# A hybrid attention and mLSTM layer on one core: the second branch gate as one group of seven half-size products

## The chip, the cores and the metric

One core of one Trainium2 chip runs the whole kernel in one launch. The metric is the device time of one execution in microseconds (us), as the median of the runs. TensorE (PE) multiplies matrices; VectorE (DVE) and ScalarE (ACT) do the elementwise work and empty TensorE's accumulators in PSUM; GpSimd (POOL) and SyncE (SP) issue DMAs here.

## The reference

One layer of a decoder with two token mixers, sequence 512, model width 1024, fp32. Cut to what matters here:

```python
u  = rms_norm(h, norm_mix_g)
z  = u @ w_in                 # q,k,v | mLSTM q,k | v | output gate ob | i, f | ga | gb
ya = moba_attention(...)      # 8 heads x 64
hb = mlstm_chunkwise(...)     # 4 heads x 128
hb = hb * rsqrt(mean(hb*hb) + EPS)           # head norm
yb = sigmoid(ob) * hb * mlstm_norm_g
merged = sigmoid(ga) * (ya @ w_proj_a) + sigmoid(gb) * (yb @ w_proj_b)
h = h + merged @ w_out
h = h + swiglu(rms_norm(h, norm_ffn_g))
out = rms_norm(h, norm_final_g)
```

The branch gates `ga` and `gb` are each 512 tokens x 1024 features, a product of `u` with 1024 columns of `w_in`.

## The kernel before

Everything is held with features on the 128 partitions and the 512 tokens along the row. An fp32 product is made of three matmuls on numbers that are split into a high part (fp32r) and a low remainder: wh·h, wl·h, wh·l. For `u` the parts are the tiles `uh` and `ul`, eight of each; the row scale of the first norm, `rb`, is applied to the products afterwards.

**Units.** The weights of the projections come in units of 128x1024 (512 KB). For each unit SP loads `raw` (L195), ScalarE copies it to `wh` (L157) and VectorE subtracts to get `wl` (L170); `split_unit` runs two units ahead of the products (`LOOK`). `fill` takes the next unit and calls `run[kind]`. The kinds stand in a fixed order: q, k, va, ob, vb, qkb, ob, then eight units `ga`, eight `gb`, eight `p` (the two branch projections), eight `wo`. A unit of `ga`, `gb` or `wo` is 24 matmuls of 128x512 into one PSUM buffer (`mm3`, L210 to L212, eight feature tiles by three products).

**Buffers in PSUM.** `mmb` gives the projection's buffers (named mm), `sb` those named s, `accb` those named acc. The steps of attention and mLSTM (scores, masks, head norms) lie between the units; a scheduler sets each engine's order by priorities.

**The gates.** `run_g` empties a product: `ga` by a ScalarE copy, `gb` by a VectorE multiply with `rb` (L561). `run_p` makes the two projections of one block of 128 features in two PSUM buffers; VectorE multiplies each with its gate (L588, L589), adds them (L592), and the sum is split to `mgh` and `mgl`. `gate(m)` (L574 and the two sigmoids on ScalarE) prepares the gates of the block that follows. `run_wo` multiplies the merged blocks with `w_out`.

**The head norm of mLSTM.** `ml_d1` copies the numerator from PSUM to `nsb` on VectorE (L1673), and squares it on ScalarE; `ml_d2` sums the squares over the partitions by two matmuls into an s buffer, scales by 2^-39 on VectorE (L1684), takes exp(-0.5 ln) on ScalarE and one Newton step on VectorE (L336 to L338).

**Weight sums for the feed-forward part.** There, products are made in Winograd's form: a 2x2 block product by seven instead of eight block products, with sums of weight blocks. Some sums are made in DRAM, each by a copy (SP, L720) and an accumulating DMA (POOL, L722), in the order of `sum_steps`; `make_sums(n)` issues them up to a count that `fill` gives for each unit. While `st["hold"]` is true (attention steps 12 to 20) none are issued. POOL also loads the mLSTM rows `R` of each head (L1603), which are read by VectorE at L1615.

## Time and profile before

| | us |
|---|---|
| median of 3 runs (lowest, highest) | 715.43 (714.92, 715.52) |
| the profiled execution | 715.64 |
| its span, first to last instruction | 713.6 |
| PE busy | 703.6, x3272 |
| DVE busy | 600.0, x986 |
| ACT busy | 438.0, x746 |
| POOL busy | 69.8, x97 |
| mean granted clock of TensorE | 0.997 |

The span is what the instructions cover; 2.04 us of the profiled execution's own time lie around it. Matmuls are pipelined: a row of 128x512 shows 0.39 us, while the next one starts 0.23 us after it. So a busy PE in a slice says that matmuls followed one another, and the distance from start to start says how fast. The same holds, with smaller differences, for VectorE and ScalarE. In the timeline a bracket at a row's end gives the idle time of the engine before it and what ended it. The span from 254.42 us to 300.10 us is the stage of the second gate; the `p` units follow, and the `wo` units start at 343.62 us.

### The profile page before, as it was taken

The page shows a single profiled execution, that of the slowest core. Times are in us where ns is not written, and L with a number is a line of the kernel's source. Part 1 is how long each engine was busy: PE and PEld are TensorE (multiplying, and loading weights), DVE is VectorE, ACT ScalarE, POOL GpSimd, SP SyncE. Part 2 cuts the span into 40 slices and gives each one's busy share as a digit, 9 for nine tenths or more (in the row PEclk, how much of TensorE's full clock was granted, in tenths as well). Part 3 has the DMA queues.
Part 4 walks back from the last instruction along what each step waited for, and adds up shares of the span by engine and source line. Part 5 has one row for each costly group of instructions (what it writes and reads, how often), then busy time and mean ns, then how long its engine had stood idle before and what let it go on. Part 6 is the DMA issues. An engine that isn't in the chain of part 4 may idle for free.

```text
span 713.6 us, 9515 instructions
## 1 busy us (share of the span) xinstructions
PE 703.6 (99%) x3272; PEld 585.8 (82%) x3272; DVE 600.0 (84%) x986; ACT 438.0 (61%) x746; POOL 69.8 (10%) x97
## 2 busy tenths in 40 slices
PE   9999999999999999999999999999999999999995
PEld 6888888887888888888888888888888888888884
DVE  6788977888998578666699887898999799797996
ACT  6634888668784446723354756566675666575665
POOL 0013010000001000000020110011002004003000
PEclk9999999999999999999999999999999999999998
DMA  9759685623159997989988667669569649869703
GB/s 326 290 189 242 207 219 173 199 78 151 60 204 244 277 297 218 275 258 269 265 253 198 218 196 216 233 178 302 198 187 278 226 136 220 312 158 272 217 0 119
DMA packets 47009, 152.69 MB, mean 214 GB/s; under 512 B 5837, under 2 KB 6229, under 8 KB 42481
## 3 DMA queue, kind: packets, MB, share of 16 engines
q1 hardware_dynamic: 36880, 117.33, 47.7%
q0 software_dynamic: 9792, 34.21, 23.5%
q8 instruction: 26, 0.43, 0.2%
q10 hardware_dynamic: 288, 0.56, 0.2%
q14 instruction: 23, 0.18, 0.1%
HBM read 130.00 MB, written 53.52 MB: 257 GB/s over the span
## 4 chain that ended last, share of the span: by engine, by line
PE 82%; DVE 12%; ACT 3%; issue 2%; DVEq 0%; ACTq 0%
PE mm L212 10%; PE mm L210 10%; PE mm L211 10%; PE mm L855 5%; PE mm L856 5%; PE mm L854 5%; PE s L855 3%; PE s L856 3%; PE s L854 3%; PE mm L1104 2%; PE mm L1102 2%; PE mm L1101 2%; PE mm L315 2%; PE acc L315 2%; PE acc L856 1%
## 5 line engine op out<-in xcount | busy, mean ns | idle before, releaser
L157 ACT ACTIVATE w<-raw 128x1024 fp32r<-128x1024 f32 (+2 forms) x107 | 108.1, 1023 | 47.7 <-PE mm L855 20.0
L829 DVE TENSOR_TENSOR w<-raw,w 128x1024 fp32r<-128x1024 f32 x70 | 84.4, 1219 | 21.3 <-ACT w L157 21.0
L157 ACT ACTIVATE wh<-raw 128x1024 fp32r<-128x1024 f32 x56 | 59.0, 1054 | 61.4 <-PE mm L211 58.7
L170 DVE TENSOR_TENSOR wl<-raw,wh 128x1024 fp32r<-128x1024 f32 x56 | 68.2, 1218 | 10.2 <-ACT wh L157 10.0
L854 PE MATMUL mm<-w,bq 128*128 128x512 f32 x160 | 62.2, 389 | 0.0
L855 PE MATMUL mm<-w,bq 128*128 128x512 f32 x160 | 62.2, 389 | 0.0
L856 PE MATMUL mm<-w,bq 128*128 128x512 f32 x160 | 62.2, 389 | 0.0
L210 PE MATMUL mm<-u,wh 128*128 128x512 f32 x128 | 50.3, 393 | 0.0
L211 PE MATMUL mm<-u,wl 128*128 128x512 f32 x128 | 50.0, 391 | 0.0
L212 PE MATMUL mm<-u,wh 128*128 128x512 f32 x128 | 50.0, 390 | 0.0
L212 PE MATMUL mm<-ul,wh 128*128 128x512 f32 x128 | 49.8, 389 | 0.0
L211 PE MATMUL mm<-uh,wl 128*128 128x512 f32 x128 | 49.8, 389 | 0.0
L210 PE MATMUL mm<-uh,wh 128*128 128x512 f32 x128 | 49.8, 389 | 0.0
L854 PEld LDWEIGHTS mm<-w,bq 128*128 128x128 f32 x160 | 30.0, 188 | 6.3
L855 PEld LDWEIGHTS mm<-w,bq 128*128 128x128 f32 x160 | 30.0, 188 | 6.3
L856 PEld LDWEIGHTS mm<-w,bq 128*128 128x128 f32 x160 | 30.0, 188 | 6.2
L1010 DVE TENSOR_TENSOR w<-raw,w 128x1024 fp32r<-128x1024 f32 x25 | 30.2, 1216 | 1.4 <-ACT w L157 1.0
L1102 PE MATMUL mm<-w,ac 128*128 128x512 f32 x80 | 31.2, 389 | 0.0
L1101 PE MATMUL mm<-w,ac 128*128 128x512 f32 x80 | 31.1, 389 | 0.0
L854 PE MATMUL s<-w,bq 128*128 128x512 f32 x80 | 31.1, 389 | 0.0
L855 PE MATMUL s<-w,bq 128*128 128x512 f32 x80 | 31.1, 389 | 0.0
L856 PE MATMUL s<-w,bq 128*128 128x512 f32 x80 | 31.1, 389 | 0.0
(438 smaller groups left out, 1917.1 us busy)
## 6 DMA issues: line engine op xcount, KB each, us to landing
raw<-in_wall_dram SPq DMA_DIRECT2D x56, 512.0 KB, 5.6
raw<-in_wgc_dram SPq DMA_DIRECT2D x30, 512.0 KB, 5.1
raw<-ws SPq DMA_DIRECT2D x30, 512.0 KB, 5.8
ws<-in_wgc_dram SPq DMA_DIRECT2D x10, 1024.0 KB, 6.9
ws<-in_wgc_dram POOLq DMA_DIRECT2D x10, 1024.0 KB, 9.3
raw<-in_wds_dram SPq DMA_DIRECT2D x15, 512.0 KB, 6.6
ws<-in_wds_dram SPq DMA_DIRECT2D x10, 512.0 KB, 7.3
ws<-in_wds_dram POOLq DMA_DIRECT2D x10, 512.0 KB, 6.7
```

Source lines behind the costliest of these rows:

```text
L157: return A.activation(out_, in_, func, **kw)
L170: V.tensor_tensor(l, src, f(h), op=ALU.subtract)
L210: st["mm"] = T.matmul(ps, wh[:, c], rh[j], start=start and j == 0, stop=False)
L211: T.matmul(ps, wl[:, c], rh[j], start=False, stop=False)
L212: T.matmul(ps, wh[:, c], rl[j], start=False, stop=stop and j == n - 1)
L829: V.tensor_tensor(l, t, f(h), op=ALU.subtract)
L854: st["mm"] = T.matmul(ps[t], bh, wh[:, d], start=first and k == 0, stop=False, skip_group_check=not first)
L855: T.matmul(ps[t], bh, wl[:, d], start=False, stop=False, skip_group_check=not first)
L856: T.matmul(ps[t], bl, wh[:, d], start=False, stop=k == 3, skip_group_check=not first)
L1010: V.tensor_tensor(w[k][1], g[k], f(w[k][0]), op=ALU.subtract)
L1101: T.matmul(ps, bh, wh[:, d], start=first and k == 0, stop=False, skip_group_check=not first)
L1102: T.matmul(ps, bl, wh[:, d], start=False, stop=False, skip_group_check=not first)
```

## The change

**The second gate.** The eight units `gb` become fourteen units `gs`, two for each of the products W11, S1, S2, W12, S3, S4, W22 of one Winograd group on blocks of half size (512 features of `u` by 512 columns, 256 tokens). A unit is 12 matmuls of 128x512 (L633 to L635), where the two halves of the tokens are stationary and the weights move, so the gate comes out with tokens on the partitions. The sums S1 to S4 of the weights are made in DRAM from the new input `wgb`: four more copies on SP and four more accumulates on POOL, at the head of `sum_steps`. `hold` is gone, and the count given to `make_sums` is another function of the unit.

**The sums of `x`.** POOL loads `x` again (`load_x`, two DMAs of 1 MB, step 20), `combine` forms the sums of its blocks (step 25: for each of four pairs one ScalarE scaling and four VectorE steps of 128x256), and `recast` overwrites a half of `uh` and `ul` after the first unit of W11, S1, S2 and W12 (each four ScalarE and four VectorE steps of 128x256).

**Out of PSUM.** The products W11, S1 and S2 are copied to SBUF by ScalarE with their scale (`rt`, `nrt`), two copies each; W12, S3 and S4 are added to these by VectorE (L658, two each); W22 is copied by ScalarE. Each of the eight results is transposed in 32x32 blocks on VectorE (L659). After S4, and again after W22, POOL writes the four transposed row groups to DRAM (L663) and reads four blocks of `gb` back (L669), which puts the features on the partitions again.

**The p units** come in the order 4, 5, 6, 7, 0, 1, 2, 3 (`PORD`). The sums of the first three are copied from PSUM by ScalarE (two copies each), and their merging is done after the third.

**The head norm.** The copy to `nsb` moves to ScalarE, the scaling by 2^-39 goes into the scale of Ln and of the Newton step, and the last head's sum of squares lies in an mm buffer.

The diff, cut:

```diff
-    u += [("gb", m) for m in range(8)]
-    u += [("p", m) for m in range(8)]
+    u += [("gs", i) for i in range(2 * len(GW))]
+    u += [("p", m) for m in PORD]
...
-            while wstate["split"] <= min(u + LOOK, NGEN - 1):
+            kind, i = UNITS[u]
+            while wstate["split"] <= min(u + LOOK + (kind == "gs"), NGEN - 1):
                 split_unit()
             pos[0] += 1
-            make_sums(st["made"] if st["hold"] else min(st["made"] + 2, 6 * (u - 17) // 7))
+            v = u if u < G0 else max(u + G0, 2 * u - 2 * len(GW)) // 2
+            make_sums(5 * (min(v, G0 + 4) - 19 + max(v - G0 - 10, 0)) // 4)
...
+    def load_x():
+        for n, c in (("A", slice(0, 4)), ("B", slice(4, 8))):
+            gs[n] = slot4(name="c" + n)
+            nc.gpsimd.dma_start(gs[n], xT[c].rearrange("k p s -> p k s"))
...
+    def combine():
+        for k in range(4):
+            x, v = gs["A"][:, k], gs["B"][:, k]
+            ng = ng1[:, k : k + 1]
+            with tc.issue_after(raw_ins(last["a"])), tc.issue_after(raw_ins(last["v"])):
+                act_(v, v, AF.Copy, scale=col(G1 + k + 4))
+                V.tensor_tensor(x[:, A_], x[:, A_], x[:, B_], op=ALU.subtract)
+            V.scalar_tensor_tensor(x[:, B_], x[:, B_], ng, v[:, B_], op0=ALU.mult, op1=ALU.add)
+            V.scalar_tensor_tensor(v[:, B_], x[:, A_], ng, v[:, B_], op0=ALU.mult, op1=ALU.subtract)
+            V.scalar_tensor_tensor(v[:, A_], v[:, B_], -1.0, v[:, A_], op0=ALU.mult, op1=ALU.subtract)
...
+    def recast(w):
+        n, c, o = {"W11": ("A", A_, B_), "S1": ("B", B_, A_), "S2": ("A", B_, B_), "W12": ("B", A_, A_)}[w]
+        for k in range(4):
+            src, h, l = gs[n][:, k, c], uh[k][:, o], ul[k][:, o]
...
+                split_hl(src, dst=(h, l))
...
+    def run_gs(i, wh, wl):
+        w, j = GW[i // 2], i % 2
...
+        for t in range(2):
+            for e in range(2):
...
+                st["mm"] = T.matmul(ps[t], q(uh), wh[:, c], start=first and k == 0, stop=False, **g)
+                T.matmul(ps[t], q(uh), wl[:, c], start=False, stop=False, **g)
+                st["gs"] = T.matmul(ps[t], q(ul), wh[:, c], start=False, stop=k == 3, **g)
...
+                act_(o, ps[t], AF.Copy, scale=nr(1, t) if w == "S1" else r(int(w == "S2"), t))
...
+                V.scalar_tensor_tensor(o, ps[t], (nr if w == "S3" else r)(h, t), o, op0=ALU.mult, op1=ALU.add)
+            V.transpose(gs["t", n][:, :, 2 * h + t, :], o.rearrange("p (b e) -> p b e", e=32))
+        if w in ("S4", "W22"):
+            d = dram.tile([S, S], F32, name=nm("gd"))
+            for q in range(4):
+                nc.gpsimd.dma_start(
+                    d.rearrange("(b i) (r x) -> r i b x", i=32, r=4)[q],
+                    gs["t", n][32 * q : 32 * q + 32].rearrange("p b x e -> p b (x e)"),
+                )
+            for m in range(4):
+                z = gz["gb", 4 * n + m] = slot(name="gb")
+                nc.gpsimd.dma_start(z, d[m * P : (m + 1) * P, :])
...
+        if m in PORD[:3]:
+            q = slot(name="pa"), slot(name="pb")
+            for t, z in zip((pa, pb), q):
+                last["g"] = act_(z, t, AF.Copy)
+            early.append((m, *q))
+            if m == PORD[2]:
+                gate(PORD[0])
+                for x in early:
+                    merge(*x)
...
-        V.tensor_copy(nsb, num)
+        act_(nsb, num, AF.Copy)
...
-        ps = sb()
+        ps = mmb() if h == 3 else sb()
...
-        V.tensor_scalar(d2, d2, 2.0**-39, None, op0=ALU.mult)
-        act_(r, d2, AF.Ln)
+        act_(r, d2, AF.Ln, scale=2.0**-39)
...
-        st["hold"] = 12 <= n <= 20
```

**Where instructions move.** On GpSimd before, the load of the last head's rows R (the last of three, R510) stands behind two other R loads, and the next weight sum behind it:

```order
L722 DMA ws332_1486<-in_wgc_dram 128x2048 [waits DMAHW2_49,DMASW1_49,PE_49]
L1603 DMA R463_2050<-scr_530 128x1792 [waits DMASW7_49,DMAHW3_49,DMASW6_49,DMAHW4_49,DMASW2_49,PE_49]
L1603 DMA R474_2114<-scr_530 128x1792 [waits DMASW3_49]
L1603 DMA R510_2281<-scr_530 128x1792 [waits DMASW4_49,DVE_49,PE_49]
L722 DMA ws534_2388<-in_wgc_dram 128x2048 [waits DMAHW7_49,DMASW5_49,PE_49]
```

After the change, at the same place of GpSimd's order, with R516 the load of the last head's rows and the sums of `wgb` those of the gate:

```order
L1758 DMA R467_2063<-scr_534 128x1792 [waits DMASW7_49,DMASW6_49,DMAHW4_49,DMASW3_49,PE_49]
L1758 DMA R478_2128<-scr_534 128x1792 [waits DMAHW2_49,DMASW4_49]
L848 DMA ws437_1923<-in_wgb_dram 128x2048 [waits DMAHW2_49,DMASW5_49,PE_49]
L848 DMA ws418_1835<-in_wgc_dram 128x2048 [waits DMAHW0_49,PE_49]
L848 DMA ws502_2206<-in_wgb_dram 128x2048 [waits DMAHW7_49,PE_49]
L1758 DMA R516_2300<-scr_534 128x1792 [waits DMASW0_49,DVE_49,PE_49]
L848 DMA ws464_2031<-in_wgc_dram 128x2048 [waits DMAHW4_49,DMASW1_49,PE_49]
```

Three accumulates of 1 MB now stand between the second and the last R load, the nearest one directly ahead of it.

On VectorE before, late in the second gate's stage, one multiply by `rb` (gb) and one weight remainder (wl) come for each unit, with the steps of the last two heads (nt, yb) between them:

```order
L170 TENSOR_TENSOR wl649_2982<-raw622_2814,wh648_2981 128x1024
L170 TENSOR_TENSOR yb642_2941<-nt581_2618,yb642_2941 128x512
L561 TENSOR_TENSOR gb647_2975<-mm646_2950,vec_74 128x512
L170 TENSOR_TENSOR yb642_2941<-nt603_2730,yb642_2941 128x512
L1698 SCALAR_TENSOR_TENSOR nt632_2885<-nt632_2885,vec_74,ob475_2120 128x512
L170 TENSOR_TENSOR wl656_3024<-raw638_2907,wh655_3023 128x1024
L170 TENSOR_TENSOR yb654_3020<-nt632_2885,yb654_3020 128x512
L1698 SCALAR_TENSOR_TENSOR nt635_2898<-nt635_2898,vec_74,ob501_2230 128x512
L561 TENSOR_TENSOR gb653_3015<-mm652_2990,vec_74 128x512
```

After the change, at the corresponding place, u24 to u29 are halves that `recast` rewrites, L658 adds a product out of PSUM, L659 is the transpose, and wl667 and wl670 are the two units of S4:

```order
L175 TENSOR_TENSOR u24_142<-cB532_2379,u24_142 128x256
L175 TENSOR_TENSOR u25_162<-cB532_2379,u25_162 128x256
L175 TENSOR_TENSOR u27_181<-cB532_2379,u27_181 128x256
L175 TENSOR_TENSOR u29_201<-cB532_2379,u29_201 128x256
L1852 SCALAR_TENSOR_TENSOR nt644_2916<-nt644_2916,vec_74,ob506_2247 128x512
L175 TENSOR_TENSOR wl667_3045<-raw652_2951,wh666_3044 128x1024
L658 SCALAR_TENSOR_TENSOR gW11630_2861<-acc664_3017,rt_379,gW11630_2861 128x512
L175 TENSOR_TENSOR yb658_3003<-nt644_2916,yb658_3003 128x512
L659 STREAM_TRANSPOSE gt668_3060<-gW11630_2861 128x16x32
L658 SCALAR_TENSOR_TENSOR gW11631_2863<-acc665_3018,rt_379,gW11631_2863 128x512
L175 TENSOR_TENSOR wl670_3066<-raw653_2953,wh669_3065 128x1024
L659 STREAM_TRANSPOSE gt668_3060<-gW11631_2863 128x16x32
```

There is no multiply by `rb` any more at this place; the four halves for W12, two sums out of PSUM and their transposes stand among the weight remainders, and nothing of mLSTM follows them.

More of the change, by code (lines that the diff above doesn't have):

```diff
@@ L50 @@
 FEAT = np.array([256 * a + 32 * WO.index(m) + j for m in range(KT) for a in range(4) for j in range(32)])
+GW = ("W11", "S1", "S2", "W12", "S3", "S4", "W22")
+PORD = (4, 5, 6, 7, 0, 1, 2, 3)
 def _unit_order():
@@ L71 @@
 NGEN = len(UNITS)
+G0 = UNITS.index(("gs", 0))
 NG = 5
@@ L193, in load_pair @@
         for u in (2 * p, 2 * p + 1):
+            kind, i = UNITS[u]
             raw[u] = blk(name="raw", raw=True)
-            nc.sync.dma_start(raw[u], wall[u])
+            if kind == "gs":
+                w, j = GW[i // 2], slice(i % 2 * D, i % 2 * D + D)
+                src = sums["gs", w] if w[0] == "S" else wgb[{"W11": 2, "W12": 3, "W22": 1}[w]]
+                nc.sync.dma_start(raw[u], src[:, j])
+            else:
+                nc.sync.dma_start(raw[u], wall[u])
         wstate["pair"] += 1
@@ L406, in proj @@
         return ps
-    st = {"made": 0, "hold": False}
+    st = {"made": 0}
     def run_qk(kind):
@@ L571, in gate @@
+    run["gs"] = run_gs
+    mgd = {}
     def gate(m):
@@ L574, in gate, with merge @@
         V.tensor_tensor(ga, ga, rb, op=ALU.mult)
-        act_(ga, ga, AF.Sigmoid)
-        act_(gb, gb, AF.Sigmoid)
+        with tc.issue_after(raw_ins(last["g"])):
+            act_(ga, ga, AF.Sigmoid)
+            act_(gb, gb, AF.Sigmoid)
+    early = []
+    def merge(m, pa, pb):
+        ga, gb = gz.pop(("ga", m)), gz.pop(("gb", m))
+        V.tensor_tensor(ga, pa, ga, op=ALU.mult)
+        turned = lambda t: t.rearrange("p (a b c) -> p b a c", a=4, b=4)
+        turned_ = lambda t: t.rearrange("p (b a c) -> p b a c", a=4, b=4)
+        V.tensor_tensor(turned_(gb), turned(pb), turned_(gb), op=ALU.mult)
+        if m != PORD[-1]:
+            gate(PORD[PORD.index(m) + 1])
+        V.tensor_tensor(turned_(ga), turned_(ga), turned(gb), op=ALU.add)
+        mgd[m] = split_hl(ga, "mg")
+        last["g"] = last["a"]
     def run_p(m, wh, wl):
-        if m == 0:
-            gate(0)
-        if m >= 4:
+        if m in PORD[4:]:
             load_xr()
@@ L584, in run_p @@
         mm3(pa, wh, wl, range(4), [t[0] for t in ya], [t[1] for t in ya], True, True)
+        if m == PORD[0]:
+            tc.add_manual_dep(raw_ins(st["first"]), raw_ins(st["gs"]).name, behind, reason="order")
         mm3(pb, wh, wl, range(4, 8), [t[0] for t in yb], [t[1] for t in yb], True, True)
         yield
-        ga, gb = gz.pop(("ga", m)), gz.pop(("gb", m))
-        V.tensor_tensor(ga, pa, ga, op=ALU.mult)
-        V.tensor_tensor(gb, pb, gb, op=ALU.mult)
-        if m < KT - 1:
-            gate(m + 1)
-        V.tensor_tensor(ga, ga, gb, op=ALU.add)
-        mgd.append(split_hl(ga, "mg"))
+        if m in PORD[:3]:
[7 more added lines that the diff above has]
+                    merge(*x)
+        else:
+            merge(m, pa, pb)
     run["p"] = run_p
@@ L844, in product @@
         def product(ps, w, o, first=False):
-            make_sums(st["made"] + (c > 0 or w in ("S4", "W22")))
+            make_sums(st["made"] + (c > 0))
             for j, (wh, wl) in enumerate(g[w]):
@@ L1415, in hybrid_layer_kernel @@
     columns(rb[0:1, :], rt.rearrange("p (j h) -> p j h", h=1))
+    ng1 = cst.tile([P, 4], F32, name="ng1")
+    V.tensor_scalar(ng1, vec[:, G1 : G1 + 4], -1.0, None, op0=ALU.mult)
+    nrt = cst.tile([P, 4], F32, name="nrt")
+    V.tensor_scalar(nrt, rt, -1.0, None, op0=ALU.mult)
     man.close()
```

134 lines of the change are left out of this document (102 added, 32 removed).

## The prediction

> **What bounds the kernel now.** I read the page's list of engines first, then the waits of TensorE, then the busy time by stretches of 10 us from 210 to 310 us, and last the timeline around the second gate.
>
> ```profile
> PE 703.6 (99%) x3272; PEld 585.8 (82%) x3272; DVE 600.0 (84%) x986; ACT 438.0 (61%) x746; POOL 69.8 (10%) x97
> ```
> ```profile
> PE s L1571 <- ACT P L162: 1.0, 2, 0.7
> PE s L231 <- DVE mask L219: 1.0, 1, 1.0
> PE acc L1021 <- DVE w L799: 0.6, 1, 0.6
> ```
>
> TensorE is busy 99% of the span, and all its waits together are 1.0 + 1.0 + 0.6 = 2.6 us. So TensorE bounds every stage, and a matmul that goes away is worth its pitch unless a new wait takes it back. How near the other engines are to taking it back is read by stage (busy time and count of PE, PEld, DVE, ACT, POOL, then the granted clock, the DMA share and GB/s):
>
> ```profile
> 210.00:220.00 10.00, 10.00 (x53) 8.67 (x52) 9.58 (x19) 7.07 (x13) 0.87 (x1) 1.00 0.84 233
> 220.00:230.00 10.00, 10.00 (x49) 8.48 (x48) 9.44 (x16) 4.97 (x9) 1.56 (x2) 1.00 0.93 272
> 230.00:240.00 10.00, 10.00 (x48) 8.33 (x48) 3.14 (x5) 3.57 (x6) 0.68 (x1) 1.00 0.91 291
> 240.00:250.00 10.00, 10.00 (x49) 8.41 (x48) 7.10 (x12) 5.13 (x9) 0.94 (x2) 1.00 1.00 257
> 250.00:260.00 10.00, 10.00 (x46) 8.32 (x45) 8.27 (x13) 4.65 (x8) 0.79 (x1) 1.00 1.01 317
> 260.00:270.00 10.00, 10.00 (x49) 8.36 (x48) 6.76 (x10) 3.48 (x5) 0.77 (x1) 1.00 1.00 267
> 270.00:280.00 10.00, 10.00 (x46) 8.25 (x45) 7.79 (x13) 6.54 (x9) 0.82 (x1) 1.00 0.92 215
> 280.00:290.00 10.00, 10.00 (x46) 8.29 (x45) 9.30 (x14) 10.00 (x19) 0.81 (x1) 1.00 0.62 193
> 290.00:300.00 10.00, 10.00 (x46) 8.28 (x45) 4.99 (x6) 5.29 (x8) 0.79 (x1) 1.00 0.96 317
> ```
>
> VectorE has 1.7 to 3.2 us idle in each 10 us from 250 to 280, and 0.7 us from 280 to 290. That is the room into which the change puts its new work.
>
> **The term for TensorE.** The gate's stage starts with the first and ends with the last but one of these rows of TensorE; the second and third are six matmuls apart:
>
> ```profile
> 254.42 0.39 PE L210 MATMUL mm<-u,wh 128*128 128x512 f32 x1
> ...
> 300.10 0.39 PE L210 MATMUL mm<-ya,wh 128*128 128x512 f32 x1
> ...
> 301.46 0.39 PE L210 MATMUL mm<-ya,wh 128*128 128x512 f32 x1
> ```
>
> The pitch is (301.46 - 300.10) / 6 = 0.2267 us, not the 0.39 us that a row shows. Eight units of 24 are 192 matmuls (43.5 us of the 45.7 us; the rest are head norms). Fourteen units of 12 are 168. **The gain is 24 x 0.2267 = 5.44 us**, all on the path. The two matmuls of the last head's sum of squares only change their buffer. The order of the matmuls up to the first product of the gate and from `wo` on is that of before but for this, so nothing else is won.
>
> **The term for VectorE in the new stage.** I lay VectorE's new order against TensorE's new times. From these rows the pitches are: TENSOR_TENSOR 128x512 0.60 (283.78 to 284.38), with a column and a third operand 0.66 (285.58 to 286.24), 128x1024 1.14 (286.24 to 287.38), transpose 0.63 (366.84 to 367.47), 128x256 0.34 (368.37 to 368.71):
>
> ```profile
> 283.78 0.69 DVE L170 TENSOR_TENSOR yb<-nt,yb 128x512 fp32r<-128x512 f32 x1
> 284.38 0.68 DVE L561 TENSOR_TENSOR gb<-mm,vec 128x512 f32<-128x512 f32 x1
> ...
> 285.58 0.74 DVE L1698 SCALAR_TENSOR_TENSOR nt<-nt,vec,ob 128x512 f32<-128x512 f32 x1
> 286.24 1.22 DVE L170 TENSOR_TENSOR wl<-raw,wh 128x1024 fp32r<-128x1024 f32 x1
> 287.38 0.68 DVE L170 TENSOR_TENSOR yb<-nt,yb 128x512 fp32r<-128x512 f32 x1
> ```
> ```profile
> 366.84 0.71 DVE L648 STREAM_TRANSPOSE ht<-xr 128x512 f32<-128x512 f32 x1
> 367.47 0.39 DVE L687 TENSOR_TENSOR v<-ut,v 128x256 f32<-128x256 f32 x1
> ...
> 368.37 0.42 DVE L688 TENSOR_TENSOR v<-ut,v 128x256 f32<-128x256 f32 x1
> 368.71 0.69 DVE L275 TENSOR_TENSOR sq<-sq,sq 128x512 f32<-128x512 f32 x1
> ```
>
> Taken out of the stage are 8 multiplies by `rb`, 4 copies `nsb` (0.60 each) and 4 scalings (about 0.40), 8.8 us. Put in are 6 more `wl` (6.8), 16 steps of `recast` (5.4), 16 of `combine` (5.4, most of them ahead of the stage in the empty stretch from 230 to 240 us), 6 sums out of PSUM (0.63 each, 3.8) and 8 transposes (5.0): 26.4 us. The average fits: the net is 17.6 us, and the seven stretches from 230 to 300 us hold 47.35 of VectorE's work, so 22.6 were idle, or 17.2 of a stage that ends 5.4 us earlier, and the last steps may run on into the p units. The order does not spread it evenly. The remainder for the second unit of S1 (wl615) cannot start before its `wh`, about 254.8 us by the row of ScalarE's copy at this place:
>
> ```profile
> 252.70 1.06 ACT L157 ACTIVATE wh<-raw 128x1024 fp32r<-128x1024 f32 x1
> 253.67 0.61 ACT L157 ACTIVATE sqh<-sqn 128x512 fp32r<-128x512 f32 x1
> ```
>
> (254.8 is 253.67 plus the 0.52 us pitch of the `nsb` copy that now stands ahead of it, and some 0.6 of what else is late.) From wl615 through wl670, the second remainder of S4, VectorE's order holds 50 instructions: 9 of 128x1024 (10.3 us), 12 of 128x256 (4.1), 29 of 128x512 or transposes (0.60 to 0.66, 17.8). Together 32.2 us, so wl670 is ready at 254.8 + 32.2 = 287.0 at best. TensorE, without stalls, comes to the second unit of S4 after 132 of the stage's matmuls, 29.9 us, and the 2.2 us of head norms: 254.42 + 32.1 = 286.5, and to the first matmul that reads wl670 at 286.7. In between VectorE also has to wait for what ScalarE and TensorE deliver: W12 leaves PSUM only when TensorE is through with it, at about 278 us, and Ln and Exp of the head norm come by way of ScalarE. **I take a stall of 1.2 us**, with 0.3 (back to back) and 5.5 (every instruction costs what its row shows, 0.08 us above its pitch, 50 x 0.08 = 4.0 us, and 1.2 of waits) as the ends. It is nearest to the back-to-back rows, because 276.50 to 288 us of before was such a run.
>
> **The term for the last head's rows.** The load of R for the last head, issued at 203.50 before, now stands behind an accumulate of 1 MB on the same queue, which waits for the end of the first ga product (the matmul at 201.55 below) and so goes out some 2 us earlier:
>
> ```profile
> 203.50 0.53 POOL L1603 DMA_DIRECT2D R<-scr  x1 [37.20 <-PE acc L1586]
> ```
> ```profile
> 209.95 1.14 DVE L1615 SCALAR_TENSOR_TENSOR R<-con,cS,R 128x128 f32<-128x128 f32 x4 [0.90 <-DMA R<-scr]
> ```
> ```profile
> 213.65 0.60 ACT L157 ACTIVATE ga<-mm 128x512 f32<-128x512 f32 x1
> ```
> ```profile
> 201.55 0.39 PE L212 MATMUL mm<-ul,wh 128*128 128x512 f32 x1
> ...
> 219.47 0.39 PE L210 MATMUL mm<-u,wh 128*128 128x512 f32 x1
> ```
> ```profile
> ws<-in_wgc_dram POOLq DMA_DIRECT2D x10, 1024.0 KB, 9.3
> R<-scr POOLq DMA_DIRECT2D x4, 896.0 KB, 6.2
> h1d<-ht POOLq DMA_DIRECT2D x8, 256.0 KB, 6.1
> ks<-sd POOLq DMA_DIRECT2D x8, 256.0 KB, 8.7
> ```
>
> VectorE already waits 0.90 us for R. Its landing moves from 209.9 to between 210 (the two share the DMA engines) and 216 us (one after the other: 201.6 + 9.3 + about 5 of the 6.2). VectorE and ScalarE then come up to 6 us late, in a stretch where VectorE has only 0.4 to 0.6 us in ten to catch up; TensorE's tightest buffer there is that of ga1, emptied at 214.25 and wanted at 219.47, 5.2 us of room. So the price is 0 to 2 us, **and I take 0.3**. [...]
>
> **The round trip of the gate.** VectorE goes on from wl670 with 9.1 us of its order to the last transpose of S4, about 297.8. Four writes on POOL at 0.67 us each (2.66 for four in the row below) end at 300.5 and land by about 306 (6.1 us each, the median of the like writes to h1d); four reads follow, landing between 309 and 311 if they are as fast as the quickest small loads, some 4 us.
>
> ```profile
> 367.85 2.66 POOL L652 DMA_DIRECT2D h1d<-ht x4 [6.90 <-DVE v L687]
> ```
>
> They are wanted by the sigmoid after the third `p` unit, three units of 24 matmuls (16.3 us) after the stage's end at 300.1 - 5.4 + 1.5 = 296.2, so at 312.5 to 314. The first half is covered by about 3 us; if that cover is gone (writes and reads at the 8.7 us of the slowest such group, `ks`) it lands at 317.8 and costs some 4 us. The second half lands near 321 and is wanted at 320.6, by ScalarE only, which is two units ahead with the weights: 0, at most 2. **I take 0 for both.**
>
> **The p units and wo.** Ten VectorE merge steps are queued ahead of the one that frees a buffer for the second sum of p0: 0.4 us, between 0 and 1.5. The last merged block is wanted nine matmuls (2.04 us) into `wo`; by these rows its sum ends at 344.55 + 0.61, 1.54 us after the start of `wo` at 343.62, and ScalarE's high part 0.6 later: 0.1.
>
> ```profile
> 343.82 0.69 DVE L589 TENSOR_TENSOR gb<-mm,gb 128x512 f32<-128x512 f32 x1 [1.69 <-PE mm L212]
> 344.55 0.69 DVE L592 TENSOR_TENSOR ga<-ga,gb 128x512 f32<-128x512 f32 x1
> ```
>
> Costed at nothing: the eight ScalarE copies out of PSUM, six more `wh` and the recasts on ScalarE (about 24 us where the seven stretches from 230 to 300 us hold 38.7 of its work and so 31.3 of idle time), the constants ng1 and nrt early on, and the eight more sum transfers, since the sums of the feed-forward part are made well ahead of their use. The last rests on the order alone; if they collide with weight loads at a DMA share of 0.9 to 1.0, up to 2 us.
>
> **The sum.** -5.44 + 1.2 + 0.3 + 0 + 0.4 + 0.1 = -3.44 us. Against the profiled execution, 715.64 (its span 713.6 and 2.04 around it), that is 712.2; the execution is 0.21 above the median of the runs, 715.43, so I forecast 712.0.
>
> **The rivals.**
> (a) *The full gain*: VectorE and the queues keep up, stalls under 0.5 us in all: 715.43 - 5.0 = 710.4, chance 0.20. For it speaks the idle time by averages; against it, that wl670 is late even back to back.
> (b) *VectorE becomes the bound of the new stage, and the kernel is slower.* From wl615 on TensorE runs at VectorE's speed. If the 50 instructions take 36 us with all their waits (32.2 at best) plus another 1 us through W22, the stall is 4.8, and with the R load at its late end (2) and 0.5 for p and wo the sum is +1.9 - that is 717.3. It decides from a stall above 6.8 us over all places. For it: the stage has 26.4 us more on VectorE; against it: the run from 276.50 to 288 us kept its pitch. Chance 0.09.
> (c) *The gate comes late by way of DRAM.* Writes and reads at the slow median of `ks`: 4 us more than the forecast, 716.0. For it: sixteen small transfers on the one queue that also carries accumulates of 9.3 us. Against it: 3 us of cover. Chance 0.11.
> [...]
>
> **Chances.** Forecast 0.57; (a) 0.20; (b) 0.09; (c) 0.11; (d) 0.03. The forecast stands for all stalls together of 0.9 to 4.0 us, 710.9 to 714.0. The range that holds the time 8 times in 10 reaches down to the whole gain of 5.44 (710.0, with 0.1 to spare) and up over (c) to 716.0, which also takes in most of VectorE's upper end; (b) and (d), 0.12, are left out. What a measurement of this kernel can tell from no change is about 0.2%, 1.4 us. Faster by more (under 714.0): 0.20 + 0.55 = 0.75. Within: 0.02 of the forecast, 0.11 of (c) and 0.02 of (b) with smaller stalls, 0.15. Slower (above 716.9): 0.07 of (b) and 0.03 of (d), 0.10.
>
> **What the profile after would show.** Right: 24 matmuls fewer at the same pitch; one new wait of TensorE on a `wl` of L175 near 287 us, of 0.5 to 2 us; VectorE above 95% from 255 to 298 us; R landing near 214 us; no wait of ScalarE for gb before the first sigmoid. Wrong: waits of TensorE on L175 over several units from 270 us on would be (b); a wait for gb on ScalarE near 313 us, followed by one of TensorE for a buffer or a merged block, would be (c); POOL rows at L663 much longer than 0.7 us would be (d); none of these waits would be (a).

## The result: 7.5 us slower, and the profile after

| | before | after |
|---|---|---|
| median (lowest, highest), us | 715.21 (714.92, 715.52) | 722.67 (722.14, 724.82) |
| the profiled execution, its span | 715.64, 713.6 | 722.58, 720.8 |
| mean granted clock of TensorE | 0.997 | 0.996 |

The ratio is 1.011, with a 95% interval from 1.0089 to 1.0131. The forecast was 712.0, with a range to 716.0 and 3 chances in 4 for faster. So it was wrong in its sign.

The list of engines of the kernel after (busy us, share of the span, instructions), and its waits of TensorE (us in total, how often, the longest):

```profile
PE 702.9 (98%) x3248; PEld 581.2 (81%) x3248; DVE 617.4 (86%) x1024; ACT 460.5 (64%) x790; POOL 84.7 (12%) x119
```
```profile
PE mm L1252 <- ACT gs L167: 1.7, 1, 1.7
PE mm L1835 <- DVE sql L175: 1.5, 1, 1.5
PE s L1726 <- ACT P L167: 1.1, 2, 0.8
PE mm L1007 <- ACT bq L162: 1.1, 1, 1.1
...
PE mm L1009 <- DVE bq L802: 0.9, 1, 0.9
PE s L367 <- DVE sql L175: 0.9, 1, 0.9
PE mm L223 <- DVE ga L689: 0.8, 1, 0.8
...
PE s L634 <- DVE wl L175: 0.6, 2, 0.4
```

The 24 matmuls are gone (3272 to 3248), but before there were three lines of waits and now there are twelve. I summed over the whole timeline of TensorE by how much the distance from one start to the next exceeds the pitch of its form: 14.4 us before, 27.0 after. That is 12.6 more, less the 5.4 won, and so 7.2, the difference of the spans. The 12.6 consist of:

| place (us) | lost, us | after what |
|---|---|---|
| up to 250 | 0.4 | small gaps |
| 264 to 267 | 2.1 | last head's sum of squares (L1834, L1835) |
| 268 to 271.3 | 1.7 | eight matmuls at 0.43 us instead of 0.23 |
| 288 and 291 | 0.9 | wl in S4 (L634) |
| 324 and 347 | 1.2 | second sum of p0, first merged blocks of wo |
| 391.7, 393.5, 410.3, 472.5 | 5.3 | start of the feed-forward part (L1007, L1009, L367, L1252) |
| the rest | 1.0 | many small gaps |

The stretches of the stage (busy time and count of PE, PEld, DVE, ACT, POOL; granted clock, DMA share, GB/s):

```profile
230.00:240.00 10.00, 10.00 (x48) 8.34 (x47) 3.95 (x7) 3.05 (x5) 0.82 (x1) 1.00 1.03 344
240.00:250.00 10.00, 9.99 (x48) 8.14 (x47) 10.00 (x23) 6.77 (x14) 0.83 (x1) 1.00 0.52 150
250.00:260.00 10.00, 10.00 (x49) 8.40 (x48) 10.00 (x19) 9.09 (x16) 0.81 (x1) 1.00 1.01 258
260.00:270.00 10.00, 8.29 (x31) 6.20 (x30) 10.00 (x16) 9.00 (x18) 0.00 (x0) 0.89 0.75 231
270.00:280.00 10.00, 10.00 (x43) 8.17 (x42) 10.00 (x17) 9.77 (x16) 1.56 (x2) 0.94 0.76 214
280.00:290.00 10.00, 9.85 (x44) 7.84 (x43) 10.00 (x17) 9.11 (x15) 0.00 (x0) 1.00 1.01 338
```

VectorE is busy without a gap from 240 us on, and idle for 6 of the 10 us before that. The steps of `combine` were to use exactly that stretch, and did not. The timelines of GpSimd, ScalarE and VectorE tell why:

```profile
227.18 0.81 POOL L590 DMA_DIRECT2D cB<-in_xT_dram  x1 [9.39 <-PE s L1791]
...
238.43 0.72 ACT L162 ACTIVATE cB<-cB,vec 128x512 f32<-128x512 f32 x1 [5.18 <-DMA cB<-in_xT_dram]
...
239.59 0.56 DVE L175 TENSOR_TENSOR Al<-R,Ah 128x384 fp32r<-128x384 f32 x1 [5.09 <-ACT Ah L162]
...
266.11 0.68 DVE L175 TENSOR_TENSOR sql<-sqn,sqh 128x512 fp32r<-128x512 f32 x1
```

The buffer for the second half of x is read by a product until 227 us (the wait in the first row), so the load lands only at 238.4. ScalarE's first step of `combine` waits 5.18 us for it; the head's `Ah`, the next in ScalarE's order, comes out behind it at 239.05, and VectorE waits 5.09 us for that. Later `sql`, which TensorE needs for the last sum of squares, comes out at the end of VectorE's unbroken queue. TensorE there:

```profile
264.82 0.50 PE L1834 MATMUL mm<-sqh,onesr 128*128 128x512 f32 x1 [0.17 <-ACT sqh L162]
266.85 0.50 PE L1835 MATMUL mm<-sql,onesr 128*128 128x512 f32 x1 [1.53 <-DVE sql L175]
267.19 0.39 PE L633 MATMUL s<-wh,u 128*128 128x512 f32 x1
...
267.92 0.63 PE L633 MATMUL s<-wh,u 128*128 128x512 f32 x1
268.35 0.63 PE L634 MATMUL s<-wl,u 128*128 128x512 f32 x1
```

Rows of 0.63 us instead of 0.39 and starts 0.43 apart instead of 0.23 are a TensorE at half its rate, with nothing to wait for; the granted clock of 0.89 and 0.94 in the two stretches above says the same.

The start of the feed-forward part, on GpSimd, ScalarE and VectorE, and the DMA groups (count, KB each, median us to landing):

```profile
372.80 0.81 POOL L848 DMA_DIRECT2D ws<-in_wgc_dram  x1 [11.24 <-PE mm L227]
373.52 2.77 POOL L777 DMA_DIRECT2D h1d<-ht  x4
...
389.80 0.63 ACT L162 ACTIVATE bq<-v 128x512 fp32r<-128x512 f32 x1 [5.69 <-DMA h1d<-ht]
...
390.46 0.69 DVE L175 TENSOR_TENSOR bq<-v,bq 128x512 fp32r<-128x512 f32 x1 [5.28 <-ACT bq L162]
```
```profile
gd<-gt POOLq DMA_DIRECT2D x8, 256.0 KB, 6.8
gb<-gd POOLq DMA_DIRECT2D x8, 256.0 KB, 4.2
h1d<-ht POOLq DMA_DIRECT2D x8, 256.0 KB, 10.4
```

Before, the four writes of h1d went out at 367.85, and an accumulate of 1 MB behind them at 372.90. Now an accumulate stands ahead of them. It is held back by its pacing (it waits for a product on TensorE, 11.24 us) until 372.80. The writes' data is there at 368.9 (the last transpose, L773), but they go out behind it, at 373.52, and land 12.3 to 14.2 us after their issue, where before it was 5.1 to 6.2 (the 10.4 of the row is the median of these four and of four later ones). ScalarE, VectorE and TensorE wait in turn.

### The profile page after: what moved, and what is told of

It reads as the page before. It is cut to its first block, busy times and chain, and to the rows that moved or that the text cites. A ratio compares the mean times of both kernels' runs of the same rounds, so it can differ in the third digit from the quotient of the medians.

```text
span 720.8 us, 9625 instructions
## 1 busy us (share of the span) xinstructions
PE 702.9 (98%) x3248; PEld 581.2 (81%) x3248; DVE 617.4 (86%) x1024; ACT 460.5 (64%) x790; POOL 84.7 (12%) x119
## 4 chain that ended last, share of the span: by engine, by line
PE 64%; DVE 19%; DMA 9%; ACT 4%; issue 3%; POOL 0%; SPq 0%; DVEq 0%; ACTq 0%; POOLq 0%
PE mm L223 5%; PE mm L227 5%; PE mm L226 5%; PE mm L1009 4%; PE mm L1008 4%; PE mm L1007 4%; DMA ws<-in_wgc_dram 2%; PE mm L1252 2%; PE mm L1255 2%; PE mm L1253 2%; PE s L1008 2%; PE s L1009 2%; PE s L1007 2%; DMA h1d<-ht 2%; DVE wl L175 2%
## 5 line engine op out<-in xcount | busy, mean ns | idle before, releaser
L175 DVE TENSOR_TENSOR wl<-raw,wh 128x1024 fp32r<-128x1024 f32 x62 | 75.0, 1216 | 15.3 <-ACT wh L162 10.9
L162 ACT ACTIVATE wh<-raw 128x1024 fp32r<-128x1024 f32 x62 | 65.1, 1055 | 31.8 <-PE mm L226 22.2
L1007 PE MATMUL mm<-w,bq 128*128 128x512 f32 x160 | 62.4, 390 | 1.1 <-ACT bq L162 1.1
L1009 PE MATMUL mm<-w,bq 128*128 128x512 f32 x160 | 62.3, 390 | 0.9 <-DVE bq L802 0.9
L223 PE MATMUL mm<-u,wh 128*128 128x512 f32 x96 | 38.0, 395 | 0.0
L227 PE MATMUL mm<-u,wh 128*128 128x512 f32 x96 | 37.5, 391 | 0.0
L226 PE MATMUL mm<-u,wl 128*128 128x512 f32 x96 | 37.4, 390 | 0.0
L227 PE MATMUL mm<-ul,wh 128*128 128x512 f32 x96 | 37.4, 389 | 0.0
L226 PE MATMUL mm<-uh,wl 128*128 128x512 f32 x96 | 37.4, 389 | 0.0
L223 PE MATMUL mm<-uh,wh 128*128 128x512 f32 x96 | 37.4, 389 | 0.0
L1007 PEld LDWEIGHTS mm<-w,bq 128*128 128x128 f32 x160 | 30.0, 188 | 7.7 <-ACT bq L162 1.5
L1009 PEld LDWEIGHTS mm<-w,bq 128*128 128x128 f32 x160 | 30.0, 188 | 7.5 <-DVE bq L802 1.4
L1252 PE MATMUL mm<-w,ac 128*128 128x512 f32 x80 | 31.3, 391 | 1.7 <-ACT gs L167 1.7
L1007 PE MATMUL s<-w,bq 128*128 128x512 f32 x80 | 31.1, 389 | 0.0
L1009 PE MATMUL s<-w,bq 128*128 128x512 f32 x80 | 31.1, 389 | 0.0
```

The source lines that it names most:

```text
L162: return A.activation(out_, in_, func, **kw)
L175: last["v"] = V.tensor_tensor(l, src, f(h), op=ALU.subtract)
L223: st["mm"] = T.matmul(ps, wh[:, c], rh[j], start=start and j == 0, stop=False)
L226: T.matmul(ps, wl[:, c], rh[j], start=False, stop=False)
L227: T.matmul(ps, wh[:, c], rl[j], start=False, stop=stop and j == n - 1)
L1007: st["mm"] = T.matmul(ps[t], bh, wh[:, d], start=first and k == 0, stop=False, skip_group_check=not first)
```

## Experiments

The theory: two transfers that come late make the loss, (1) the accumulate ahead of the h1d writes, about 5 us, and (2) the late second half of x, which makes ScalarE and VectorE stand and sends VectorE into the stage without room, 2 to 4 us. The rivals: the loss is VectorE's amount of work in the stage, wherever it stands; or it is the head norm's new form. Ratios are to the kernel before, measured beside it on the same chip, with 95% intervals.

**1. `combine` one step later**, when its data is there.

```diff
-        20: [load_x()], 25: [combine()],
+        20: [load_x()], 26: [combine()],
```

> The changed kernel with combine() one step later (step 26 instead of 25), nothing else. Theory 1, the late half of x: in the changed kernel ScalarE stood 5.2 us before 238.43 us waiting for cB, the second half of the reloaded x, and VectorE 5.1 us behind it, so VectorE came to the gate's stage with no room left (busy 10.00 of every 10 us from 240 to 300); with the later step that wait goes, the last head's sum of squares is ready in time, and the 2.1 us wait of TensorE near 265 us, the slow matmuls behind it (1.7 us) and most of the waits for wl near 288 and 291 us (0.9) go: 718 to 719.5 us, with the waits at the start of the feed-forward part (5.3 us) still there. Theory 2, too much work: VectorE has more work in the stage than time, and the wait near 265 us only moves to another place: 721.5 to 723.5 us.

Measured: 720.91, ratio 1.0082 [1.0051, 1.0113]. ScalarE's wait for x, the wait at the last head's sum and the slow matmuls behind it are gone. But the waits for wl in the stage grew from 0.9 to 2.5 us (1.10, 0.56 and 0.80, at 279, 285 and 289 us): late matmuls had given VectorE time that it now lacks. About 2 us were won by the medians, less than expected. (The edit does not bring all of `combine` ahead of the stage: half of it now comes between 242 and 246 us, half between 256 and 262.)

**2. No accumulate ahead of the h1d writes** (changed kernel; all sums of the p and wo units move into the feed-forward part).

```diff
-            make_sums(5 * (min(v, G0 + 4) - 19 + max(v - G0 - 10, 0)) // 4)
+            make_sums(5 * (min(v, G0 + 4) - 19) // 4)
```

> The changed kernel, where no weight sum is issued in the p and wo units; they go out later, in the feed-forward part. Theory 1, the queue: four writes of h1d stand on GpSimd behind an accumulate that is held back until 372.8 us, then share the queue with its 1 MB, and land 14 us after their issue; without it they go out near 369 us and land in about 6 us, and the waits of TensorE at 391.7, 393.5, 410.3 and 472.5 us (1.2 + 1.1 + 1.1 + 1.9 = 5.3 us) go: 717 to 718.5 us. Theory 2, lateness handed on: those waits come from VectorE and ScalarE, which are still behind from the gate's stage, and the time stays at 721.5 to 723.5 us; or the sums that are made later hold up the feed-forward part in their turn, with waits of TensorE for weights after 500 us.

Measured: 717.28, ratio 1.0027 [1.0018, 1.0037], 5.4 us less than the changed kernel by spans and by medians. All four waits of the feed-forward part are gone. GpSimd's row, its DMA group, and the stretch of the head norm:

```profile
369.36 2.66 POOL L777 DMA_DIRECT2D h1d<-ht  x4 [42.64 <-DVE ht L773]
```
```profile
h1d<-ht POOLq DMA_DIRECT2D x8, 256.0 KB, 5.6
```
```profile
260.00:270.00 10.00, 8.28 (x36) 6.26 (x35) 10.00 (x17) 9.21 (x18) 0.00 (x0) 1.00 0.77 240
```

The writes now wait for nothing but their data, and these four land in 3.4 to 5.4 us. The third row shows the same 1.53 us wait of TensorE as the changed kernel, but a granted clock of 1.00: no slow matmuls followed. The time came back in part as a wait for wl, 1.23 us at 281.

**3. Both edits.**

> Both edits of the two runs before together. Theory 1 (two separate waits on GpSimd's queue, each with its own cost): the gains add, 713 to 715 us, TensorE's waits no more than some 3 us longer in all than in the kernel before the change. Theory 2 (VectorE has too much work in the gate's stage, the rest is handed on): 720 us or more.

Measured: 714.91, ratio 0.9989 [0.998, 0.9999]. So the two edits together take back the whole 7.5 us, and no more: of the 5.4 us won on TensorE nearly all is still given back. TensorE's waits in the stage and at the second sum of p0:

```profile
PE s L634 <- DVE wl L175: 1.0, 2, 0.6
...
PE mm L634 <- DVE wl L175: 0.9, 1, 0.9
PE mm L223 <- DVE ga L689: 0.8, 1, 0.8
```

From start to start they cost 2.5 us (wl) and 0.9 us (p0); 0.2 at `wo` and some 1.6 of small gaps make up the rest.

**4. The head norm alone**, in the kernel before: `nsb` on ScalarE, 2^-39 in Ln and in the Newton step, an mm buffer for the last head.

```diff
-        V.tensor_copy(nsb, num)
+        act_(nsb, num, AF.Copy)
-        ps = sb()
+        ps = mmb() if h == 3 else sb()
-        V.tensor_scalar(d2, d2, 2.0**-39, None, op0=ALU.mult)
-        act_(r, d2, AF.Ln)
+        act_(r, d2, AF.Ln, scale=2.0**-39)
```

> The kernel before with only the head norm's part of the change: nsb copied by ScalarE, the 2^-39 folded into Ln and the Newton step, the last head's sum of squares in a projection buffer. TensorE had room everywhere there, so both theories give no difference, 714.5 to 716 us; a third theory, that this part brought the wait near 265 us (by its buffer or by the copy on ScalarE), gives 717 us or more with a wait of TensorE at that sum of squares.

Measured: 715.42, ratio 0.9996 [0.9987, 1.0006]. The same three waits of 1.0, 1.0 and 0.6 us as before. The head norm's new form costs nothing; that rival falls.

**5. Eight multiplies out of VectorE's queue** (kernel 3, `ga` times `rb` moved behind the last transpose of W22).

```diff
-        V.tensor_tensor(ga, ga, rb, op=ALU.mult)
...
+            with tc.issue_after(raw_ins(last["t"])):
+                for k in PORD:
+                    V.tensor_tensor(gz["ga", k], gz["ga", k], rb, op=ALU.mult)
```

> The kernel of e3 (combine one step later, no sums in p and wo) with the eight multiplications of ga by rb moved on VectorE behind the last transpose of W22, where it waits for ScalarE; four of them (4 x 0.60 = 2.4 us) stood between 247 and 262 us. Theory 1, VectorE has more work than time between 250 and 300 us: the three waits of TensorE for wl near 279, 285 and 289 us (2.5 us together in e3) shrink by about 2 us, 712.3 to 713.5 us. Theory 2, these waits come from ScalarE's order (wh late) or from the reading of PSUM: no difference, 714.3 to 715.5 us.

Measured: 714.84, ratio 0.999 [0.9981, 1.0]. A miss: the waits for wl are 0.92, 0.53 and 0.80, hardly less, and a new one of 1.3 us (L223, for `mgh`) stands at `wo`. The multiplies had stood ahead of 260 us, where ScalarE and TensorE pace VectorE: it gains 0.8 us of idle time from 250 to 260 us (9.24 us busy), and no room later.

**6. x earlier, the sums later** (the changed kernel with another count; both halves of x were to come before the stage).

```diff
-            make_sums(5 * (min(v, G0 + 4) - 19 + max(v - G0 - 10, 0)) // 4)
+            make_sums(min(5 * (u - 19) // 4, 12) + max(5 * (min(v, G0 + 8) - G0 + 2) // 4, 0))
```

> The changed kernel with combine at its own place (step 25), no sums in p and wo as in e2, and the weight sums held at twelve while x is loaded again (units 30 to 34), so that only the accumulate for S4 is ahead of the two loads on GpSimd's queue. Theory 1, x came late because the sums shared the queue and the DMA engines: the second half lands 3 us or more earlier than at 238.4 us, ScalarE's wait of 5.2 us falls under 2 us, and the time is 713 to 715 us, as in e3 or better. Theory 2, the load is late because its buffer comes free only at 227 us: it is issued and lands as before, and the time is that of e2, 716.5 to 718 us.

Measured: 733.55, ratio 1.0253 [1.0238, 1.0269], a miss on the other side. The load of the second half went out at 227.87, no earlier, since its buffer comes free only then; it landed at 236.3. And the moved sums put an accumulate just ahead of the gate's own writes. GpSimd's timeline, the DMA group, and TensorE's largest wait:

```profile
297.95 0.79 POOL L848 DMA_DIRECT2D ws<-in_wds_dram  x1 [4.82 <-PE mm L634]
299.18 2.66 POOL L663 DMA_DIRECT2D gd<-gt  x4 [0.44 <-DVE gt L659]
...
313.67 2.17 POOL L669 DMA_DIRECT2D gb<-gd  x4 [11.83 <-DMA gd<-gt]
```
```profile
gd<-gt POOLq DMA_DIRECT2D x8, 256.0 KB, 11.7
```
```profile
PE mm L223 <- DVE ga L689: 5.8, 1, 5.8
```

The writes land in 11.7 us where they took 6.8. ScalarE waits 12.9 us for the gate, TensorE 5.8 us for the merged sum behind it. This is what the prediction's rival (c) would look like. It is only in part a second case of the first cause of the loss: the four writes behind the accumulate take 10.7 us (7.4 in the changed kernel), but the four of the gate's second half, with no accumulate ahead of them, take 11.1 (6.2), and the DMA engines are 98% busy or more in each 4 us from 296 to 328. Another 7 us are lost from 598 to 608 us, where TensorE waits 3.0 and 0.8 us for weights of the feed-forward part and then runs at half rate; what made these late was not followed.

**7. The same with the multiplies of experiment 5.**

> e6 with the multiplications of ga by rb moved as in e5. If VectorE's work between 240 and 300 us is what is left, it gains 1.5 to 3 us on e6: 711 to 713 us. If not, it stays at e6's time.

Measured: 731.73, ratio 1.0239 [1.0222, 1.0256]: 1.8 us under experiment 6 by the medians, with intervals that overlap. TensorE's waits for wl in the stage fell from 2.0 us (0.89, 0.57 and 0.56) to one of 0.57. In experiment 6 VectorE is busy all the time from 240 us on, so here, other than in experiment 5, the multiplies leave a stretch that is full.

**8. The changed kernel once more**, unchanged, to see how constant its waits and its slow matmuls are.

> The changed kernel as it is, one more look, for the slow matmuls. In its profile TensorE ran eight matmuls at 0.43 us from start to start (267.9 to 270.9 us, the granted clock 0.89 in that stretch) right behind the wait of 2.1 us near 265 us; e2 has the same wait and no slow matmuls. If the wait brings them on, they are there again, and TensorE waits little for wl near 281 us; if they come by chance, they are gone or elsewhere, and TensorE waits about 1.2 us for wl near 281 us instead, as in e2, at the same total.

Measured: 725.63 in one execution, span 723.9, granted clock 0.992. The same wait of 1.53 us at 265 us, and no slow matmuls behind it; but there were some at other places, after the waits of 0.95 and 0.94 us at the feed-forward part's start (393.11 and 394.79 us). The stretch of these two waits and the one behind it, where ten matmuls take 3.41 us at a granted clock of 0.50:

```profile
391.96:395.38 3.42, 1.53 (x6) 0.79 (x6) 3.42 (x7) 1.58 (x2) 0.00 (x0) 1.00 0.53 131
395.38:398.79 3.41, 3.41 (x10) 2.67 (x9) 3.41 (x6) 1.20 (x2) 0.00 (x0) 0.50 0.01 2
```

The same came again from 477.8 to 481 us, after a wait of 2.7 us at L1252. So the wait of 1.53 us at 265 us was followed by eight matmuls at half rate in one execution of this kernel, and by none in this one.

**9. Less work on VectorE in the stage**: kernel 3 without the low parts of the recast for S2 and W12, 8 instructions of 128x256 or 2.7 us. The low part of these two products is left out, so the gate is not the reference's.

```diff
-            else:
+            elif w == "S1":
...
+            else:
+                act_(h, src, AF.Copy)
```

> The kernel of e3 where VectorE's half of recast for S2 and W12 is left out (the low parts of these halves of u stay what they were, so gate B is not that of the reference): eight steps of 128x256, 2.7 us of VectorE's work, are gone from the stretch in which e3 and e5 still wait 2.5 us for wl; ScalarE's work is unchanged. Theory 1, the fixed number of VectorE's instructions between the remainder of S1 and that of S4 sets these waits: they fall to 0.5 us or less and the time by about 2 us on e3, 712.5 to 713.5 us. Theory 2, ScalarE's high parts set them: no change, 714.4 to 715.4 us.

Measured: 712.16, ratio 0.9955 [0.9937, 0.9973]. One wait of 0.6 us for wl is left:

```profile
PE mm L636 <- DVE wl L175: 0.6, 1, 0.6
```

The kernel is 3.43 us below the one before (715.59 beside it), kernel 3 was 0.76 below: 2.7 us by the medians for 2.7 us of VectorE's work. In the two traces TensorE's lost time in the stage falls by 2.1 us, from 2.7 to 0.6. In this stage VectorE's work counts nearly one for one.

**10. The sums of the fourth p unit copied by ScalarE too** (kernel 3), against the 0.9 us at p0.

```diff
-        if m in PORD[:3]:
+        if m in PORD[:4]:
```

> The kernel of e3 with the sums of the fourth p unit also copied out of PSUM by ScalarE, while the merging still begins after the third. Theory 1: TensorE's wait of 0.8 us (0.9 with the restart) at the second sum of p0 comes from the buffer that VectorE frees behind ten merge steps; it goes, 713.7 to 714.5 us. Theory 2: ScalarE's two more copies delay the sigmoids and the high parts of the merged blocks, and the wait comes back at the start of wo: 714.6 to 715.5 us.

Measured: 717.23, ratio 1.0026 [1.0016, 1.0036]. A miss: the copy stands behind the sigmoids on ScalarE, TensorE waits 2.6 us for its buffer there, and seven matmuls at half rate follow (325.9 to 328.9 us).

**11. The last two heads' yb behind all units of the gate** (kernel 10).

> The kernel of e10 with the last steps of mLSTM heads 2 and 3 (scaling by the output gate and split of yb, 2.5 us of VectorE's work) placed behind the transposes of S4 instead of among the weight remainders. Theory 1, VectorE's work between 260 and 290 us is what TensorE waits for: the waits for wl fall by about 2 us, of which up to 1.3 us may come back at the second sum of the first p unit, which reads yb: 711.5 to 713.5 us. Theory 2, ScalarE or PSUM set these waits: 714 to 715 us, or more by the new wait.

Measured: 719.91, ratio 1.0066 [1.005, 1.0082]. The last two waits for wl are gone, but ScalarE's copy of yb, ahead of the copies of W22, waits 2.5 us for VectorE, and TensorE 3.0 us for the buffer of W22, with 14 slow matmuls behind. The wait of 2.6 us that experiment 10 brought is still there.

**12. The recast for W12 one unit later** (kernel 3).

```diff
-            if w in ("W11", "S1", "S2", "W12"):
-                recast(w)
+            if w in ("W11", "S1", "S2", "S3"):
+                recast("W12" if w == "S3" else w)
```

> The kernel of e3, complete, with recast for W12 done one product later (after the first unit of S3; only W22 reads it), so four VectorE steps of 128x256 (1.4 us) and four of ScalarE move behind the remainder of the second unit of S4. Theory 1, the order of VectorE's work among the remainders sets the waits: of the three waits for wl (1.1, 0.6 and 0.8 us with restart) the last two go, 713.4 to 714.2 us. Theory 2, the total of VectorE's work in the stage sets them, wherever it stands: the waits move to W22 or to the p units and the time stays at 714.5 to 715.3 us.

Measured: 714.59, ratio 0.9989 [0.998, 0.9998]. From start to start the waits are 1.10 at 279 us, 0.73 at 288 and 0.82 at 292 (the last for a buffer that VectorE empties): 2.65, the same total in other places.

**13. And the next step of the last heads one unit later** (kernel 12 with one more `fill(1)` ahead of the loop of `ml_e`).

> The kernel of e12 with the last steps of the four mLSTM heads (ml_e) issued one unit later, so that one step of 128x512 more stands behind each of the remainders that TensorE waits for. Theory 1: the first wait for wl (1.1 us near 279 us) goes or shrinks to 0.5 us too, 712.5 to 713.5 us. Theory 2: no gain over e3, or a new wait of TensorE for yb at the first p unit or for a PSUM buffer that ScalarE frees late, 715 us or more.

Measured: 714.30, ratio 0.9985 [0.9976, 0.9993]. Waits of 1.15 and 1.43 us, again 2.6. What is moved inside the stage moves the wait, not its sum.

**14. Four of `combine`'s sixteen VectorE steps made earlier**: the differences of the first half of x, which is there at step 25; the rest at step 26 (kernel 13). Two of the four stood in the stage, near 256 us.

```diff
+    def differ():
+        for k in range(4):
+            x = gs["A"][:, k]
+            with tc.issue_after(raw_ins(last["a"])), tc.issue_after(raw_ins(last["v"])):
+                V.tensor_tensor(x[:, A_], x[:, A_], x[:, B_], op=ALU.subtract)
...
-        25: [combine()],
+        25: [differ()], 26: [combine()],
```

> The kernel of e13, complete, with the four differences of cA that combine needs (128x256 each, 1.35 us of VectorE's work in all; they read the first half of the reloaded x alone) made one step earlier, in VectorE's idle stretch before 240 us. Theory, VectorE bounds the gate's stage from about 247 us on: the two differences that stood near 255 us (0.7 us) leave it, and so does the time, 713.3 to 713.9 us; the other two stood before an idle 0.9 us at 246.6 and win nothing. Rival, the waits that are left in e13 (2.4 us for wl and for a product's buffer) are set by ScalarE or by PSUM: 714.0 to 714.6 us.

Measured: 713.47, ratio 0.9969 [0.9957, 0.9981]. This computes the whole layer and is faster than both kernels, by 2.1 us against the one before (715.53 beside it). Against experiment 13 (1.35 below the one before) that is 0.7, as forecast for the two steps that left the stage, but the intervals overlap and the two traces have the same span, 712.3: this last step is not shown. The stretch from 230 us in experiment 3 and here, and TensorE's waits behind it:

```profile
230.00:240.00 10.00, 10.00 (x49) 8.33 (x48) 6.93 (x13) 5.45 (x9) 0.82 (x1) 1.00 1.02 342
```
```profile
230.00:240.00 10.00, 10.00 (x48) 8.36 (x47) 8.55 (x17) 4.94 (x9) 0.82 (x1) 1.00 1.01 344
```
```profile
PE mm L639 <- ACT wh L162: 1.0, 1, 1.0
...
PE mm L223 <- DVE ga L695: 0.8, 1, 0.8
```

VectorE's work in the stretch was 3.95 us in the changed kernel. The later `combine` made it 6.93, since VectorE no longer stands there, and the four steps make it 8.55. All waits for wl are gone. One wait of 1.17 us from start to start is left at the last product, and the p0 wait of 0.93.

## Why the prediction was wrong, step by step

**Right.** TensorE's term: 24 matmuls fewer and, where nothing waits, the same pitch. The load of R: here the timelines of GpSimd and VectorE answer to the rows of before.

```profile
201.86 0.81 POOL L848 DMA_DIRECT2D ws<-in_wgb_dram  x1 [14.61 <-PE mm L227]
203.38 0.58 POOL L1758 DMA_DIRECT2D R<-scr  x1 [0.71 <-PE acc L1741]
...
215.94 1.14 DVE L1770 SCALAR_TENSOR_TENSOR R<-con,cS,R 128x128 f32<-128x128 f32 x4 [5.36 <-DMA R<-scr]
```

R is there at 215.9, the late end of the 210 to 216 forecast (203.38 + 12.56, where before it was 6.45), and TensorE did not wait for it. On GpSimd's queue the accumulate of 201.86 lands after 9.9 us, at 211.8, and R 4.1 us behind it; the one of 372.80 lands after 11.0, at 383.8, and the four writes of h1d behind it, from 385.8 to 389.7. The gate's round trip cost nothing: its writes land in 6.8 us, its reads in 4.2, and ScalarE waits 0.4 us for it. p and wo took 0.93 and 0.25 us where 0.4 and 0.1 were taken (the first had 1.5 as its end). The longer rows at L663 that would have been rival (d) did not come: four writes take 2.67 us, where the like ones took 2.66 before, in a VectorE that is busy all the time.

**The step that failed, 5.3 us.** "Costed at nothing: … the eight more sum transfers, since the sums of the feed-forward part are made well ahead of their use." They are; no use of a sum was late in the changed kernel. What counts is what stands behind the accumulate on GpSimd's queue: four small writes that are wanted at once, behind an instruction that waits for its pacing. They go out 4.6 us after their data is there, and take some 8 us longer to land, behind the accumulate's 1 MB. The end of that paragraph, "up to 2 us", was put down to a collision with weight loads, not to this. The step looked at the readers of what it moved, and did not look past the moved instruction in the new order, where the h1d writes stand behind it. Experiment 2 settles it: without the sums in the p and wo units, −5.4 us, and all four waits are gone.

**The second step that failed, 3.8 us where it bites.** "16 of `combine` (5.4, most of them ahead of the stage in the empty stretch from 230 to 240 us)." In the kernel before, VectorE is idle in that stretch because it waits for `wh` (3.09 us) and for a sum on TensorE (3.77 us). In the changed kernel ScalarE and VectorE stand there for the data that `combine` needs. The load's issue was taken from its place in the order, not from when its buffer comes free (227 us), and the data lands at 238.4, when the stretch is over. At the last head's sum this costs 2.1 us and the half rate behind it 1.7; what experiment 1's edit wins in all is 1.8 us by the medians (2.4 from experiment 2 to 3), since the stage takes a part of it back.

**The mis-sized term.** "I take a stall of 1.2 us", with 0.3 and 5.5 as ends. In the changed kernel it is 0.9, but only since TensorE had come 3.8 us late by itself. Where that is mended it is 2.5 (experiments 1 and 3). The count of VectorE's work was right: the 50 instructions from wl615 to wl670 take 32.05 us, as good as the 32.2 back to back. Their first and last:

```profile
259.89 1.22 DVE L175 TENSOR_TENSOR wl<-raw,wh 128x1024 fp32r<-128x1024 f32 x1
...
290.81 1.21 DVE L175 TENSOR_TENSOR wl<-raw,wh 128x1024 fp32r<-128x1024 f32 x1
```

What was wrong is the start: 254.8 was taken, and it is 259.89, 5.1 us late, with VectorE's stand of 5.09 us ahead of it. So wl670 is ready at 291.9 and not at 287.0. In experiment 3 the run starts on time, but it is longer, since eight steps of `combine` and two more of `recast` stand in it: 59 instructions in 35.4 us.

```profile
254.52 1.22 DVE L175 TENSOR_TENSOR wl<-raw,wh 128x1024 fp32r<-128x1024 f32 x1
...
288.78 1.21 DVE L175 TENSOR_TENSOR wl<-raw,wh 128x1024 fp32r<-128x1024 f32 x1
```

So this term failed by the second step too: the work that was to be done ahead of the stage is done in it. By experiments 9, 12 and 13 the total of VectorE's work in the stage sets the wait, and not its place there. Rival (b) has TensorE wait for VectorE over several units, as the runs showed; but it had the instructions take longer than their pitch, and what happened is that they began late or were more. (Its stall of 4.8 us also leaves out the 0.3 that wl670 is late even back to back; with it the sum would be +2.2 and not +1.9.)

**Not foreseen, 0 to 1.7 us for most waits.** Half rate of TensorE after a wait: below.

The sign came from the first two; without them the kernel comes to 714.91 (experiment 3), inside the range, but within what can be told from no change. So the first two are shown by taking them out; how the 1.6 us of small gaps that are left in experiment 3 arise, and what would remove the p0 wait of 0.9 us (experiment 10 did not), stays open.

## What to carry to other kernels

For every DMA that a change adds or moves, read what stands behind it in its engine's order, and whether a wait that is only there for pacing holds it (here 11.24 us, and 5.3 us of TensorE's time); the readers of its own data were the lesser question here. For every reload, find when its buffer comes free before an empty stretch is counted as room: here the data landed at 238.4 us, when the stretch from 230 to 240 was nearly over, and the engines that waited for it, 5.18 and 5.09 us, kept the work behind it waiting too. And ask whether an engine is full over a whole stage: here VectorE was, its work counted nearly one for one (2.7 us less of it won 2.7 us by the medians), and moving it about inside the stage only moved the wait (2.65 and 2.6 us).
